# Second parts of 36 weight slabs: an accumulating DMA in place of a VectorE subtraction

## Chip, cores and metric

One core of one Trainium2 chip runs the whole program. The metric is device time in microseconds (us), as the median of several runs; a profile comes from one further execution.

## What is computed

Two residual blocks act on 256 tokens of width 1024, in float32. The first is a gated linear attention, a convolutional feed-forward, an attention and a second feed-forward. The second block, where the change lies, is cut here to what matters:

```
h = rmsnorm(x) * (1 + scale) + shift
c_val, c_gate, c_og, ts, r_og, g_conv, g_rwkv = split(h @ w_in)
y_conv = (silu(layernorm(conv31(c_val * sigmoid(c_gate)))) * silu(c_og)) @ w_conv_out
y_rwkv = (norm(rwkv7_scan(r, k, v, ... from ts)) * silu(r_og)) @ w_rwkv_out
m = sigmoid(g_conv) * y_conv + sigmoid(g_rwkv) * y_rwkv
x = x + gate * (m @ w_out);  return rmsnorm(x)
```

## The kernel before

**Split weights.** A weight matrix comes in slabs of 128 x 1024 (512 KB). `Weights.load` (L67) loads a slab into `raw` by a DMA that SP issues (L76), ACT rounds it to float32r as `hi` (L77), and DVE makes the remainder `lo = raw - hi` (L78). `mm3` (L107) then issues three matmuls for each of the 8 blocks of a slab: `hi` with the activations' first part (L110), `hi` with their second part (L111), and `lo` with their first part (L112). A slab is 24 matmuls. The third of them already needs `lo`.

**Buffers.** The pools ask for five `raw` tiles (L1239) and three each of `hi` and `lo` (L1240); the build hands out more where SBUF is free. In the addresses of the built programs, slabs of `w_r` and `w_k` reuse the `lo` of four (before) or five (changed) slabs earlier, those of `w_v` and of the gates the one of three slabs earlier.

**Stages of the second block.** `low` and `cvg` are projections; `pr`, `pk` and `pv` project `w_r`, `w_k`, `w_v` (8 slabs each). `prep` builds the scan's chunk matrices. `inv` inverts 32 x 32 triangular blocks on DVE: two transposes (L799), 31 steps of a multiplication (L618, tile `sub`) and an addition (L808), and transposes back (L817, L819). After them TensorE goes on with `zp` (L829), `xp` (L839) and `chain`, four chunks of small matmuls (`u`, `sp`, `op`, `ur`) with copies on ACT and additions on DVE between them and two norms (`ost`, L911). The last stages are `rout`, `cout`, `wout` and `final`.

**What fills the gaps.** Slabs of the gates `rog`, `gr`, `cog` and `gc` (8 each) are given to `prep`, `inv` and `chain` as filler by `fill`, and the 248 taps of the 31-wide convolution (L1017, L1019) fill DVE. `gr`, `cog` and `gc` leave for DRAM through `kept` (an ACT activation, L943, and a DMA that ACT issues, L944) and come back later; `rog` stays in SBUF. The framework's list scheduler sets the order on every engine from its own costs, and each engine works through its order without overtaking. The lines before and after the change differ by five from L78 on (L829 is L834 there).

Of the kernel before, what the change touches and what calls it, by code (L numbers as in the profile page):

```python
# [12 lines left out]
AF = mybir.ActivationFunctionType  # L13
ALU = mybir.AluOpType
# [3 lines left out]
P = 128  # L18
# [40 lines left out]
class Weights:  # L59
# [5 lines left out]
        self.last = None  # L65
        self.ready = {}

    def load(self, src, out=None):

        g, nc = self.g, self.g.nc  # L70
        w, n = src.shape[-1], self.n
        self.n += 1
        raw = g.wraw.tile([P, 1024], F32, tag="raw", name=f"raw{n}")
        hi, lo = out or [g.wsp.tile([P, 1024], F32R, tag=a, name=f"{a}{n}") for a in ("hi", "lo")]
        with g.tc.issue_after(self.last.ins):
            self.last = nc.sync.dma_start(raw[:, :w], src)  # L76
        nc.scalar.copy(hi[:, :w], raw[:, :w])  # L77
        nc.vector.tensor_tensor(out=lo[:, :w], in0=raw[:, :w], in1=hi[:, :w].bitcast(F32), op=ALU.subtract)  # L78
        return hi[:, :w], lo[:, :w]
# [10 lines left out]
        self.last = self.g.nc.sync.dma_start(raw, src)  # L90
        return raw.rearrange("p (k c) -> p k c", c=P)

    def blocks(self, src, n):

        w = self.ready.pop(str(src), None) or self.load(src)
        return [a.rearrange("p (k c) -> p k c", c=n) for a in w]

    def ahead(self, where, i):
# [9 lines left out]
def mm3(nc, ps, lhs, rhs, start, stop):  # L108
    (lh, ll), (rh, rl) = lhs, rhs
    nc.tensor.matmul(ps, lh, rh, start=start, stop=False)  # L110
    nc.tensor.matmul(ps, lh, rl, start=False, stop=False)  # L111
    nc.tensor.matmul(ps, ll, rh, start=False, stop=stop)  # L112
# [63 lines left out]
def scaled(g, w_col, name, wide=T):  # L176

    nc = g.nc
    hh = g.sb.tile([P, KD, wide], F32R, tag=f"ph{wide}", name=f"ph_{name}")
    hl = g.sb.tile([P, KD, T], F32R, tag="pl", name=f"pl_{name}")  # L180
    for k in range(KD):
        nc.scalar.activation(hh[:, k, :T], g.x[:, k, :], AF.Copy, scale=w_col[:, k:k + 1])
        nc.vector.scalar_tensor_tensor(out=hl[:, k, :], in0=g.x[:, k, :], scalar=w_col[:, k:k + 1], in1=hh[:, k, :T].bitcast(F32), op0=ALU.mult, op1=ALU.subtract)
    return hh, hl
# [8 lines left out]
def normed(g, w_col, rstd, name, shift=None):  # L193

    nc = g.nc
    hh, hl = [g.sb.tile([P, KD, T], F32R, tag=t, name=f"{t}_{name}") for t in ("hh", "hl")]
    for k in range(KD):
        h = g.sb.tile([P, T], F32, tag="e", name=f"h_{name}{k}")
        nc.vector.scalar_tensor_tensor(out=h, in0=g.x[:, k, :], scalar=w_col[:, k:k + 1], in1=rstd, op0=ALU.mult, op1=ALU.mult)
        if shift is None:  # L200
            split_act(g, h, hh[:, k, :], hl[:, k, :])
        else:
            s = shift[:, k:k + 1]
            nc.scalar.activation(hh[:, k, :], h, AF.Identity, bias=s)
            nc.vector.scalar_tensor_tensor(out=hl[:, k, :], in0=h, scalar=s, in1=hh[:, k, :].bitcast(F32), op0=ALU.add, op1=ALU.subtract)
    return hh, hl
# [48 lines left out]
        nc.vector.tensor_tensor(out=g.x[:, c, :], in0=ps[:, :T], in1=g.x[:, c, :], op=ALU.add)  # L255


def projecting(g, src, h, evac, first=0, hp=None):


    nc = g.nc
    for c in range(src.shape[0]):
        wh, wl = g.w.blocks(src[c], P)
        ps = g.pj.tile([P, 512], F32, tag="pj", name=f"pj{g.w.n}")
        n = T + 2 if c < first else T
        for k in range(KD):
            if c < first:
                nc.tensor.matmul(ps[:, :n], wh[:, k, :], hp[0][:, k, :n], start=k == 0, stop=False)
                nc.tensor.matmul(ps[:, :T], wh[:, k, :], hp[1][:, k, :], start=False, stop=False)
                nc.tensor.matmul(ps[:, :n], wl[:, k, :], hp[0][:, k, :n], start=False, stop=k == KD - 1)  # L270
            else:
                mm3(nc, ps[:, :T], (wh[:, k, :], wl[:, k, :]), (h[0][:, k, :], h[1][:, k, :]), k == 0, k == KD - 1)
        evac(c, ps[:, :n])
        yield


def project(*a, **k):
    for _ in projecting(*a, **k):
        pass
# [310 lines left out]
def head_rows(g, r, name):  # L590

    nc = g.nc
    ps = g.po.tile([16, T], F32, name=f"hr_{name}")
    for t in range(2):
        nc.tensor.transpose(ps[:, t * P:(t + 1) * P], r[:, t, :], g.cst["ident"])
    out = [g.sb.tile([16, T], F32R, tag=f"hr{i}", name=f"hr{i}_{name}") for i in range(2)]
    split_act(g, ps, *out)
    return out
# [15 lines left out]
def second(g, order):  # L614
    nc, I, cst = g.nc, g.I, g.cst
# [9 lines left out]
    hp = scaled(g, wn, "s", T + 32)  # L625
# [3 lines left out]
    h = normed(g, wn, rstd, "s", shift=g.mod)  # L629
# [8 lines left out]
    wl = sb.tile([65, T], F32, name="wl")  # L638
    al = sb.tile([64, T], F32, name="al")
    nc.gpsimd.memset(wl, 1.0)  # L640
    v = Ctx()

    def shift_mix(ps, c, out):
        nc.scalar.activation(out, ps, AF.Copy, scale=mu1[:, c:c + 1])
        nc.vector.scalar_tensor_tensor(out=out[:, 1:], in0=ps[:, :T - 1], scalar=mu[:, c:c + 1], in1=out[:, 1:], op0=ALU.mult, op1=ALU.add)

    def heads(name, after=None):
        v.hexp = sb.tile([16, D], F32R, name="hexp" + name)
        hx = sb.tile([16, D], F32, tag="hx", name="hx" + name)
        with g.tc.issue_after(g.w.last.ins if after is None else after.ins):  # L650
            nc.sync.dma_start(hx, I["hexp"])
        nc.scalar.copy(v.hexp, hx)
# [30 lines left out]
    def pair():  # L683
        if not hasattr(v, "qr"):
            v.qr = sb.tile([P, KD, 2, T], F32, name="qr")

    def pk():
        pair()
        st = psum.tile([P, 2, 16], F32, name="kst")

        def ev(j, ps):
            k = v.qr[:, j, 0, :]
            shift_mix(ps, 8 + j, k)
            sq = sb.tile([P, T], F32, tag="kksq", bufs=LAG + 1, name=f"kksq{j}")
            nc.scalar.activation(sq, k, AF.Square, scale=cst["k_k"][:, j:j + 1])
            sqs.append((j, sq))
            if len(sqs) > LAG:
                norms()

        def norms():  # L700
            j, sq = sqs.pop(0)
            for t in range(2):
                nc.tensor.matmul(st[:, t, 2 * j:2 * j + 2], sq[:, t * P:(t + 1) * P], cst["hind"], start=True, stop=True)

        sqs = []
        project(g, I["w_k"], h, ev)
        while sqs:
            norms()
        heads("k")
        v.rs = head_rows(g, rsqrt(g, st, 1e-24, None, "kk"), "kk")  # L710

    def pr():
        pair()
        project(g, I["w_r"], h, lambda j, ps: shift_mix(ps, j, v.qr[:, j, 1, :]))

    def pv():
        v.VU = sb.tile([P, 4, 16, 64], F32, name="VU")
        v.vf = full("vf")

        def ev(j, ps):  # L720
            vj = v.vf[:, j, :]
            shift_mix(ps, 16 + j, vj)
            vt = psum.tile([P, 4, P], F32, name=f"vt{j}")
            for c in range(4):
                nc.tensor.matmul(vt[:64, c, :], vj[:, c * 64:(c + 1) * 64], cst["center"], start=True, stop=True)
            nc.scalar.copy(v.VU[:64, :, 2 * j:2 * j + 2, :], vt[:64].rearrange("p c (h v) -> p c h v", h=2))

        project(g, I["w_v"], h, ev)


    def prep():
# [199 lines left out]
    def kept(name, src, f):  # L931

        if name not in SPILL:
            t = full(name)
            setattr(v, name, lambda j: t[:, j, :])
            setattr(v, name + "t", t)
            yield from projecting(g, src, h, lambda j, ps: nc.scalar.activation(t[:, j, :], ps, f))
            return
        d = g.dram.tile([P, KD, T], F32, name=name + "d")

        def ev(j, ps):
            t = sb.tile([P, T], F32, tag="spill", bufs=2, name=f"{name}o{j}")
            nc.scalar.activation(t, ps, f)  # L943
            nc.scalar.dma_start(d[:, j, :], t)  # L944

        def get(j):
            t = sb.tile([P, T], F32, tag=name + "i", name=f"{name}i{j}")
            g.w.after(t, d[:, j, :])
            return t

        setattr(v, name, get)
        yield from projecting(g, src, h, ev)

    gates = dict(gr=kept("gr", I["w_gr"], AF.Sigmoid), gc=kept("gc", I["w_gc"], AF.Sigmoid),
                 cog=kept("scog", I["w_cog"], AF.Silu), rog=kept("srog", I["w_rog"], AF.Silu))

# [107 lines left out]
    def wout():  # L1064
# [3 lines left out]
        def ev(j, ps):  # L1068
            nc.vector.scalar_tensor_tensor(out=g.x[:, j, :], in0=ps, scalar=g.mod[:, 16 + j:17 + j], in1=g.x[:, j, :], op0=ALU.mult, op1=ALU.add)

        (project if isinstance(v.mh, list) else project_plain)(g, I["w_out"], v.mh, ev)

    steps = dict(low=low, pk=pk, pr=pr, pv=pv, prep=prep, inv=inv, chain=chain, gains=gains, cvg=cvg, conv=conv, cln=cln,
                 rout=rout, cout=cout, wout=wout)
    for n in order.split():
# [230 lines left out]
```

## Time and profile before

| what | value |
|---|---|
| median of 3 runs | 1025.53 us (1023.55 to 1026.45) |
| profiled execution | 1027.12 us |
| its span, first to last instruction | 1025.3 us |
| TensorE busy | 990.1 us, 97% |
| VectorE busy | 799.8 us, 78% |
| ScalarE busy | 602.8 us, 59% |
| GpSimd busy | 8.4 us, 1% |
| slab DMAs of `w_gr` | 512 KB each, 3.3 us to landing |

The profiled execution has 1.8 us outside its span, and lies 1.6 us above the median of the runs. A busy share is an average over all stages. What a part of the change is worth is read from the stage where it lies: a table of stretches, then the waits and the order of time within one stretch.

### The profile page before, as it was taken

The numbers are of one execution on the slowest core, as the hardware profiler recorded it, in microseconds if no ns is written. First come the engines' busy times: TensorE is split into PE (matmuls) and PEld (weight loads), VectorE is DVE, ScalarE is ACT, GpSimd is POOL, SyncE is SP. The second block draws the span as 40 slices with busy tenths as digits, with TensorE's granted clock in tenths as the row PEclk, the third lists the DMA queues.
The fourth block names the chain that finished last, engine by engine and source line by source line (L and its number), as shares of the span: only waits on it lengthen the run. The fifth ranks groups of instructions, "written<-read, shape, count | busy, mean of one in ns | idle before, by whom it ended". The sixth has DMA issues, their size and how long they took to land. (4 is left out here: it accounts for less than half of the span.)

```text
span 1025.3 us, 20257 instructions
## 1 busy us (share of the span) xinstructions
PE 990.1 (97%) x8124; PEld 940.7 (92%) x8124; DVE 799.8 (78%) x1521; ACT 602.8 (59%) x1057; POOL 8.4 (1%) x19
## 2 busy tenths in 40 slices
PE   6799999999999999899999999999999999999996
PEld 6788899999999878899999998999988898888996
DVE  6765589888876697888887558999898999774674
ACT  7744667666544577656665446545559764634453
POOL 0000000000000000000000000000000100000000
PEclk9899999999999999989999999999999999889998
DMA  7537256556676652365555665455322267313741
GB/s 290 184 131 263 76 175 206 185 187 184 211 258 229 240 189 86 141 205 186 177 187 154 188 243 203 145 185 167 124 85 81 81 222 235 112 37 109 265 161 41
DMA packets 54157, 175.06 MB, mean 171 GB/s; under 512 B 6288, under 2 KB 12944, under 8 KB 53680
## 3 DMA queue, kind: packets, MB, share of 16 engines
q1 hardware_dynamic: 50320, 169.51, 49.8%
q10 hardware_dynamic: 3744, 4.27, 1.2%
q8 instruction: 63, 1.03, 0.4%
q14 instruction: 30, 0.25, 0.1%
HBM read 168.51 MB, written 5.24 MB: 169 GB/s over the span
## 5 line engine op out<-in xcount | busy, mean ns | idle before, releaser
L78 DVE TENSOR_TENSOR lo<-raw,hi 128x1024 fp32r<-128x1024 f32 (+2 forms) x278 | 332.2, 1203 | 28.5 <-ACT hi L77 24.1
L77 ACT CAST hi<-raw 128x1024 fp32r<-128x1024 f32 (+2 forms) x278 | 281.8, 1030 | 41.5 <-PE pj L111 28.5
L112 PE MATMUL up<-hh_f,lo 128*128 128x256 f32 x640 | 182.3, 285 | 2.6 <-DVE lo L78 2.4
L110 PE MATMUL up<-hh_f,hi 128*128 128x256 f32 x640 | 182.4, 285 | 0.8 <-ACT hi L77 0.8
L111 PE MATMUL up<-hl_f,hi 128*128 128x256 f32 x640 | 182.2, 285 | 0.0
L110 PE MATMUL pj<-hh_s,hi 128*128 128x256 f32 x544 | 158.6, 292 | 0.0
L111 PE MATMUL pj<-hl_s,hi 128*128 128x256 f32 x544 | 157.3, 289 | 0.0
L112 PE MATMUL pj<-hh_s,lo 128*128 128x256 f32 x544 | 156.9, 289 | 0.0
L112 PEld LDWEIGHTS up<-hh_f,lo 128*128 128x128 f32 x640 | 124.0, 194 | 3.1 <-DVE lo L78 3.0
L110 PEld LDWEIGHTS up<-hh_f,hi 128*128 128x128 f32 x640 | 124.1, 194 | 1.0 <-ACT hi L77 1.0
L111 PEld LDWEIGHTS up<-hl_f,hi 128*128 128x128 f32 x640 | 124.1, 194 | 0.0
L110 PEld LDWEIGHTS pj<-hh_s,hi 128*128 128x128 f32 x544 | 106.1, 195 | 1.8 <-issue 0.8
L111 PEld LDWEIGHTS pj<-hl_s,hi 128*128 128x128 f32 x544 | 106.3, 195 | 1.0 <-issue 0.3
L112 PEld LDWEIGHTS pj<-hh_s,lo 128*128 128x128 f32 x544 | 106.2, 195 | 1.1 <-issue 0.5
L1019 DVE SCALAR_TENSOR_TENSOR y<-u,long,y 128x255 f32<-128x255 f32 (+27 forms) x240 | 100.1, 473 | 0.2
L110 PE MATMUL dn<-gh,hi 128*128 128x256 f32 x352 | 99.4, 283 | 0.0
L112 PE MATMUL dn<-gh,lo 128*128 128x256 f32 x352 | 99.4, 283 | 0.0
L111 PE MATMUL dn<-gl,hi 128*128 128x256 f32 x352 | 99.4, 283 | 0.0
L238 ACT ACTIVATE y<-up,const 128x256 f32<-128x256 f32 x80 | 45.2, 566 | 51.1 <-PE up L112 46.6
L111 PEld LDWEIGHTS dn<-gl,hi 128*128 128x128 f32 x352 | 67.5, 192 | 0.0
L110 PEld LDWEIGHTS dn<-gh,hi 128*128 128x128 f32 x352 | 67.5, 192 | 0.0
L112 PEld LDWEIGHTS dn<-gh,lo 128*128 128x128 f32 x352 | 67.5, 192 | 0.0
(463 smaller groups left out, 1960.0 us busy)
## 6 DMA issues: line engine op xcount, KB each, us to landing
raw<-w_up SPq DMA_DIRECT2D x88, 512.0 KB, 3.5
raw<-w_down SPq DMA_DIRECT2D x32, 448.0 KB, 3.8
adaw<-ada_w SPq DMA_DIRECT2D x24, 512.0 KB, 4.6
raw<-w_down SPq DMA_DIRECT2D x16, 512.0 KB, 4.5
raw<-w_cvg SPq DMA_DIRECT2D x16, 512.0 KB, 3.4
raw<-gla_v SPq DMA_DIRECT2D x8, 512.0 KB, 5.4
raw<-gla_g SPq DMA_DIRECT2D x8, 512.0 KB, 4.2
raw<-gla_out SPq DMA_DIRECT2D x8, 512.0 KB, 5.0
```

Source lines behind the costliest of these rows:

```text
L77: nc.scalar.copy(hi[:, :w], raw[:, :w])
L78: nc.vector.tensor_tensor(out=lo[:, :w], in0=raw[:, :w], in1=hi[:, :w].bitcast(F32), op=ALU.subtract)
L110: nc.tensor.matmul(ps, lh, rh, start=start, stop=False)
L111: nc.tensor.matmul(ps, lh, rl, start=False, stop=False)
L112: nc.tensor.matmul(ps, ll, rh, start=False, stop=stop)
L238: nc.scalar.activation(yb, ps[:, b, :], AF.Identity, scale=cw[:, 1, c:c + 1], bias=cw[:, 3, c:c + 1])
L1019: nc.vector.scalar_tensor_tensor(out=y[:, i:], in0=u[:, :T - i], scalar=w[:, j, 30 - i:31 - i], in1=y[:, i:], op0=ALU.mult, op1=ALU.add)
```

## The change

In 36 of the 89 split slabs of the second block `lo` is made another way: ACT writes the slab, negated and rounded to float32r, into `lo`, and a DMA issued by POOL (GpSimd) adds `raw` to it. The rounded negative is `-hi`, so the sum is the same remainder. ACT still makes `hi`. With `acc=2` it is every second slab of `w_k`, `w_r` and `w_v` (12), with `acc=1` every slab of those gates that `kept` spills, `gr`, `cog` and `gc` (24). `rog`, which stays in SBUF, and all other slabs keep the subtraction.

```diff
-    def load(self, src, out=None):
+    def load(self, src, out=None, acc=False):
...
             self.last = nc.sync.dma_start(raw[:, :w], src)
+        if acc:
+            nc.scalar.activation(lo[:, :w], raw[:, :w], AF.Copy, scale=-1.0)
+            nc.gpsimd.dma_start(lo[:, :w], raw[:, :w], accum_op=ALU.add)
+            nc.scalar.copy(hi[:, :w], raw[:, :w])
+            return hi[:, :w], lo[:, :w]
         nc.scalar.copy(hi[:, :w], raw[:, :w])
...
-def projecting(g, src, h, evac, first=0, hp=None):
+def projecting(g, src, h, evac, first=0, hp=None, acc=0):
...
-        wh, wl = g.w.blocks(src[c], P)
+        wh, wl = g.w.blocks(src[c], P, acc > 0 and c % acc == acc - 1)
...
-        project(g, I["w_k"], h, ev)
+        project(g, I["w_k"], h, ev, acc=2)
...
-        yield from projecting(g, src, h, ev)
+        yield from projecting(g, src, h, ev, acc=1)
```

`w_r` and `w_v` get `acc=2` in the same way.

The scheduler's order moves with it. On DVE, in the middle of `inv` (`sub` and `LT` are its steps, `y` a convolution tap), before:

```order
L618 TENSOR_TENSOR sub_9448<-LT 128x192
L78 TENSOR_TENSOR lo_9768<-raw_9766,hi_9767 128x1024
L808 TENSOR_TENSOR LT<-LT,sub_9448 128x24x8
L1019 SCALAR_TENSOR_TENSOR y<-u,long,y 128x241
L618 TENSOR_TENSOR sub_9483<-LT 128x207
L1019 SCALAR_TENSOR_TENSOR y<-u,long,y 128x240
L808 TENSOR_TENSOR LT<-LT,sub_9483 128x23x9
L78 TENSOR_TENSOR lo_9837<-raw_9835,hi_9836 128x1024
```

and now:

```order
L623 TENSOR_TENSOR sub_9460<-LT 128x192
L1024 SCALAR_TENSOR_TENSOR y<-u,long,y 128x233
L813 TENSOR_TENSOR LT<-LT,sub_9460 128x24x8
L1024 SCALAR_TENSOR_TENSOR y<-u,long,y 128x232
L623 TENSOR_TENSOR sub_9495<-LT 128x207
L1024 SCALAR_TENSOR_TENSOR y<-u,long,y 128x231
L813 TENSOR_TENSOR LT<-LT,sub_9495 128x23x9
L1024 SCALAR_TENSOR_TENSOR y<-u,long,y 128x230
```

Between the transposes of `inv` there were 19 subtractions and 41 taps; now there are no subtractions and 49 taps. On TensorE, 473 slab matmuls stood between the last matmul of `prep` and the first of `zp`; now there are 311 (46 of `rog`, 265 of spilled gates, some 11 slabs). The other 162 stand among the steps of `chain`, which had 149 and has 311.

On ACT, three gate slabs (`gro` is the gate's output, `grd` its place in DRAM), before:

```order
L943 ACTIVATE gro_10004<-pj_9979 128x256
L944 DMA grd<-gro_10004 128x256
L77 CAST hi_10191<-raw_10190 128x1024
L943 ACT_TABLE_LOAD
L943 ACTIVATE scogo_10082<-pj_10057 128x256
```

and now:

```order
L948 ACTIVATE gro_9814<-pj_9789 128x256
L78 ACTIVATE lo_9994<-raw_9992 128x1024
L80 CAST hi_9993<-raw_9992 128x1024
L949 DMA grd<-gro_9814 128x256
L80 CAST hi_10072<-raw_10071 128x1024
L948 ACTIVATE gro_9884<-pj_9859 128x256
L78 ACTIVATE lo_10073<-raw_10071 128x1024
```

The negation of a slab stands behind the gate activation of the slab three earlier, whose end frees its `lo`. On TensorE, around the first `ost` of `chain`, before:

```order
L886 MATMUL op_10354<-qr,S_10136 64x64 x16
L856 MATMUL ur_10472<-S_10351,qr 64x64
L856 MATMUL ur_10473<-S_10351,qr 64x64
...
L911 MATMUL ost_10424<-long,gsq_10422 128x2 x8
```

and now:

```order
L891 MATMUL op_10380<-qr,S_10158 64x64 x16
L115 MATMUL pj_10421<-hh_s,hi_10415 128x256
L116 MATMUL pj_10421<-hl_s,hi_10415 128x256
L117 MATMUL pj_10421<-hh_s,lo_10416 128x256
...
L916 MATMUL ost_10451<-long,gsq_10449 128x2 x8
```

Fifteen slab matmuls now stand directly ahead of it, as they already do ahead of the second `ost` of the kernel before.

## Rows read from the trace of the kernel before

**Rows 1.** The page's busy time of each engine.

```profile
PE 990.1 (97%) x8124; PEld 940.7 (92%) x8124; DVE 799.8 (78%) x1521; ACT 602.8 (59%) x1057; POOL 8.4 (1%) x19
```

**Rows 2.** Table of stretches of the second block.

```profile
core 0: us, PE busy (x) PEld busy (x) DVE busy (x) ACT busy (x) POOL busy (x), PEclk, DMA share, GB/s
650.00:757.00 107.00, 107.00 (x882) 104.71 (x880) 101.20 (x204) 53.44 (x80) 0.00 (x0) 1.00 0.48 162
...
811.00:869.00 58.00, 56.85 (x473) 56.65 (x473) 57.92 (x128) 32.53 (x48) 0.00 (x0) 1.00 0.66 206
...
872.50:940.60 68.10, 66.81 (x1026) 60.67 (x1026) 42.67 (x88) 30.96 (x53) 0.00 (x0) 0.85 0.22 71
...
876.00:882.30 6.30, 6.30 (x31) 6.01 (x30) 6.30 (x17) 5.29 (x8) 0.00 (x0) 0.51 0.69 220
...
904.00:912.20 8.20, 8.20 (x57) 7.17 (x58) 4.75 (x13) 5.64 (x9) 0.00 (x0) 0.50 0.21 65
912.20:940.60 28.40, 28.01 (x355) 25.02 (x355) 14.58 (x31) 8.48 (x17) 0.00 (x0) 0.99 0.14 46
```

**Rows 3.** Waits from 811 to 872: who waited for whom, total us, times, longest.

```profile
ACT hi L77 <- PE pj L111: 21.6, 15, 1.7
...
PE zp L829 <- DVE X L817: 2.4, 1, 2.4
```

**Rows 4.** The chain that ended last, around `zp` and the end of `chain`.

```profile
872.45 3.62 PE zp L829 x124
...
876.58 0.21 PE pj L112
...
940.64 4.37 PE pj L289 x19
```

**Rows 5.** DVE's groups of instructions from 810 to 872.4.

```profile
L78 DVE TENSOR_TENSOR lo<-raw,hi 128x1024 fp32r<-128x1024 f32 x19 | 23.1, 1218 | 0.0
```

**Rows 6.** DVE in order of time within `inv`: start, us, instruction.

```profile
833.60 1.21 DVE L78 TENSOR_TENSOR lo<-raw,hi 128x1024 fp32r<-128x1024 f32 x1
834.74 0.40 DVE L808 TENSOR_TENSOR LT<-LT,sub 128x240 f32<-128x240 f32 x1
835.06 0.45 DVE L1019 SCALAR_TENSOR_TENSOR y<-u,long,y 128x236 f32<-128x236 f32 x1
835.43 0.40 DVE L618 TENSOR_TENSOR sub<-LT 128x247 f32<-128x247 f32 x1
...
868.32 4.08 DVE L817 STREAM_TRANSPOSE X<-LT 32x1024 f32<-32x1024 f32 x2
```

**Rows 7.** The last matmul of `prep`, tile `nl`: ns min/median/max, first and last start.

```profile
L782 PE MATMUL nl<-VU,lk x128: 218/218/267, 765.7 to 810.7; 64*64 64x64 f32 x128
```

**Rows 8.** ACT in order of time, one gate slab.

```profile
829.01 0.38 ACT L943 ACTIVATE gro<-pj 128x256 f32<-128x256 f32 x1
829.41 0.33 ACTq L944 DMA_DIRECT2D grd<-gro  x1
830.93 1.05 ACT L77 CAST hi<-raw 128x1024 fp32r<-128x1024 f32 x1 [1.55 <-PE pj L111]
```

**Rows 9.** DMA queue of SP (MB, share of 16 engines), and issues with us to landing.

```profile
q1 hardware_dynamic: 50320, 169.51, 49.8%
...
raw<-w_gr SPq DMA_DIRECT2D x8, 512.0 KB, 3.3
raw<-w_cog SPq DMA_DIRECT2D x8, 512.0 KB, 4.8
...
raw<-w_out SPq DMA_DIRECT2D x8, 512.0 KB, 7.1
```

**Rows 10.** ACT's copy behind each `w_v` slab, tile `vt`: first and last start.

```profile
L726 ACT COPY VU<-vt x8: 579/580/583, 730.5 to 760.6; 64x512 f32<-64x512 f32 x8
```

**Rows 11.** TensorE in order of time: the two `ost` of `chain`.

```profile
901.40 2.49 PE L911 MATMUL ost<-long,gsq 128*128 128x2 f32 x16 [0.83 <-ACT gsq L908]
...
928.68 1.90 PE L911 MATMUL ost<-long,gsq 128*128 128x2 f32 x16
```

More of the change, by code (lines that the diff above doesn't have):

```diff
@@ L91, in plain, with blocks @@
         return raw.rearrange("p (k c) -> p k c", c=P)
-    def blocks(self, src, n):
-        w = self.ready.pop(str(src), None) or self.load(src)
+    def blocks(self, src, n, acc=False):
+        w = self.ready.pop(str(src), None) or self.load(src, acc=acc)
         return [a.rearrange("p (k c) -> p k c", c=n) for a in w]
@@ L713, in pr @@
         pair()
-        project(g, I["w_r"], h, lambda j, ps: shift_mix(ps, j, v.qr[:, j, 1, :]))
+        project(g, I["w_r"], h, lambda j, ps: shift_mix(ps, j, v.qr[:, j, 1, :]), acc=2)
     def pv():
@@ L726, in ev @@
             nc.scalar.copy(v.VU[:64, :, 2 * j:2 * j + 2, :], vt[:64].rearrange("p c (h v) -> p c h v", h=2))
-        project(g, I["w_v"], h, ev)
+        project(g, I["w_v"], h, ev, acc=2)
     def prep():
```

## The prediction

> **What bounds the kernel now.** The first view is the page's busy time [rows 1]: TensorE works 97% of the span, VectorE (DVE) 78%. That alone says that a relief of DVE pays only where TensorE waits for DVE. The second view, the table of stretches [rows 2], looks for such places in the second block. From 650 to 757 us (`w_r`, `w_k` and half of `w_v`) TensorE has no idle time at all, though DVE too is busy 101.2 of 107 us. From 811 to 869 it runs 473 slab matmuls in 56.85 us, 0.12 us each or 2.88 us per slab, at full clock, beside a DVE that is busy 57.92 of 58.00 us. Both engines are full there. The waits of that stretch [rows 3] show two things. ACT waits 15 times, 21.6 us in all, for TensorE before it writes a `hi`: the buffers of a gate slab come free only when TensorE ends an earlier slab. And TensorE waits once for DVE, 2.4 us, for the transposes that end `inv`. From there the chain that ended last [rows 4] goes through `zp` at 872.45 and the chunks of `chain` to the first large group of `rout` at 940.64. In those 68.1 us TensorE is idle for only 1.3 us [rows 2]. So little idle time is to be had anywhere: TensorE's work is only moved about, and what else can be won is clock. In two pieces, 876 to 882.3 and 904 to 912.2, the granted clock is 0.51 and 0.50, which is the lower level (1.2 GHz): a slab matmul comes every 0.21 us [rows 4].
>
> **DVE in `inv`.** The 19 subtractions leave [rows 5]. In the stream one takes 833.60 to 834.74, 1.14 us, and a tap 835.06 to 835.43, 0.37 us [rows 6]. Eight more taps stand there now. 19 x 1.14 - 8 x 0.37 = 18.7 us: the transposes end at 853.7 in place of 872.4, and `zp` can begin 18.7 us earlier if TensorE is there by then. The 12 subtractions that leave `w_r`, `w_k` and `w_v` are worth nothing: TensorE is full in that stretch [rows 2], and their place is taken by taps.
>
> **TensorE ahead of `zp`.** `prep` ends at 811 [rows 7]. Behind it stand 46 matmuls of `rog`, 46 x 0.12 = 5.5 us, and about 11 spilled slabs. With three buffers, the time from the end of a slab to its buffer being ready again, L, sets the pace: (L + 2.88) / 3 per slab if that is above 2.88, so from L = 5.76 on.
>
> **L, which no row shows.** After a slab ends, ACT does the gate activation (0.38 us) and the negation; the cast of the same shape on ACT takes 1.05 us [rows 8], and I take that. Then POOL issues the DMA; handing over to it has no row, and I put it between 0 and 1 us, and take 0.3. The DMA itself is bounded from below by the load of the same 512 KB, 3.3 us for `w_gr` [rows 9]. From above: it must read `lo` besides `raw`, so at worst it is as two transfers one after the other in a crowded stage, 7.1 (`w_out`) and 4.8 (`w_cog`), 11.9 us. In engine time a slab is 0.498 x 1025.3 us / 169.51 MB x 0.524 MB = 1.6 us of all 16 DMA engines [rows 9]. The nearest case is one landing and a second reading, 3.3 + 1.6 = 4.9 us. L = 0.38 + 1.05 + 0.3 + 4.9 = 6.6 us, the pace is 3.16 us, and 5.5 + 11 x 3.16 = 40.3 us put TensorE at 851.3, just ahead of DVE's 853.7. So this wait is covered by `inv`, with 2.4 us to spare; from L = 7.3 on `zp` is late, and if that cover is gone altogether it costs 11 x 0.28 = 3.1 us.
>
> **The other 12.** In `w_r` and `w_k` five buffers give 4 x 2.88 = 11.5 us, above 6.6. In `w_v` a slab comes every (760.6 - 730.5) / 7 = 4.3 us [rows 10], and three buffers give 8.6 us. Both are taken at 0. POOL's own work (memsets and small copies) stands ahead of the 24 gate DMAs, so nothing on POOL waits behind them. SP issues the next load of a `raw` later, when the accumulation has read it; five buffers at 2.88 us cover that.
>
> **`chain`.** The 162 moved matmuls cost 162 x 0.12 = 19.4 us there. Against that, fifteen of the slab matmuls now stand ahead of the first `ost`. Before, TensorE waited 0.83 us at that place for ACT, and behind it came the 8.2 us at half clock; ahead of the second `ost` 15 slab matmuls stood already, there was no wait [rows 11], and the clock stayed at 0.99 [rows 2]. I take both as removed: 0.8 us, and half of 8.2, 4.1 us. ACT gets nine more casts and some 13 negations in `chain`, about 22 x 1.05 = 23 us, where it is busy 31.0 of 68.1 us [rows 2]. Its copies for the scan can stand behind one of them; with ten such copies that is 0 to 10 us, and I take 2, since TensorE has slabs to do meanwhile.
>
> **Sum.** -18.7 + 19.4 - 0.8 - 4.1 + 2.0 = -2.2 us against the profiled execution of 1027.1 us. That execution lies 1.6 us above the median of the runs; the same difference on the median gives 1025.5 - 2.2 = **1023.3 us**. The rest of the program is unchanged: after 940 TensorE has the same work in the same order. No change is what a measurement can't tell within about 0.3%, 3.1 us here.
>
> **A rule that speaks against it.** From 811 to 869 the DMA engines are already busy 0.66 of the time [rows 2]. In the 42.7 us that are left ahead of `zp`, 11 loads and 11 accumulations of 1.6 us each take 35 us, and with the second reading 53 us. The Trainium skill ("DMA: Bandwidth & Descriptors", section on issuing engines not being separate DMA queues) says that DMAs issued by SP, ACT and POOL all run on the same 16 engines and interleave. By that rule the accumulations take their time from the loads, and the time is that of the first rival below; by the landings of the loads alone it is the 1023.3 above. No row here has a DMA of POOL in it.
>
> **Rivals.**
> - **The DMA engines fill, and `lo` comes late (slower).** Landing 3.3 + 4.8 = 8.1 us, L = 9.8, pace 4.2: 5.5 + 11 x 4.2 = 51.7 us, so `zp` at 862.7, 9.0 us later than DVE allows; in `w_v` (9.8 - 8.6) / 2 x 4 = 2.4 us. -2.2 + 9.0 + 2.4 = +9.2: **1034.7 us**. It decides from L = 7.3. For it: the 53 us of engine time above. Against: the loads land in 3.3 us at that load. At the upper bound of 11.9 us (L = 13.6, pace 5.5) TensorE needs 66.0 us in place of 42.7 ahead of `zp`, 23.3 us more, with 10 in `w_v` and some 8 in `w_r` and `w_k`: +39 us, 1064 us.
> - **The clock stays up in all of `chain` (faster).** With twice the slabs between the small matmuls, the 6.3 us at half clock behind `zp` go as well, and ACT costs nothing: -2.2 - 3.2 - 2.0 = -7.4: **1018.1 us**. For it: the full clock from 912 on. Against: `zp` with its 128 tiny matmuls still comes first, behind a wait for DVE.
> - **The moved slabs only stand in front of `chain` (slower).** Pieces of 36 to 48 matmuls now stand ahead of steps of the scan. If the low clock stays and ACT's extra work costs 4 us: -18.7 + 19.4 + 4.0 = +4.7: **1030.2 us**.
> - **It does nothing**: the remainder is made by either engine in time and the order makes up for it. That is within the forecast.
>
> **Chances.** The forecast has 0.45 with a spread of some 4 us: 0.14 of it faster by over 0.3%, 0.27 within, 0.04 slower. Late `lo`: 0.30 (0.28 slower, 0.02 within). Clock: 0.18, faster. Slabs in front: 0.07, slower. Together faster 0.32, within 0.29, slower 0.39. The range goes from 1017 (just below the clock's case) to 1043; above that lies about a third of the late `lo`, whose landing would be near its upper bound, and below it the best of the clock's case. The forecast's own range is 1019 to 1028.
>
> **What would show it.** Right: the transposes of `inv` end near 854, `zp` starts with them, 36 DMAs of POOL land in about 5 us, TensorE waits little for them, and the clock from the first `ost` on is full. Wrong: TensorE's waits for POOL's DMAs are the longest in the table of waits; a gate slab takes 4 us or more; loads of `w_cog` land later than 4.8 us; `chain` from `zp` to `rout` takes well over 68.1 + 16.5 = 84.6 us.

## The result, and the profile after

The changed kernel takes **1054.7 us** (median of 4 runs, 1049.6 to 1056.8) against 1025.7 us of the kernel before on the same chip (4 runs, 1023.6 to 1026.5). The ratio is **1.0273**, 95% interval 1.0251 to 1.0294: slower, and outside the range that was given. The profiled execution took 1055.9 us, its span is 1054.1 us, 28.8 us above that of before.

The page of the changed kernel, to be held against [rows 1] and [rows 9]: busy time, then TensorE's third matmul of a slab with the idle time ahead of it, then the DMA queues (packets, MB, share of 16 engines), then issues with their median time to landing.

```profile
PE 999.6 (95%) x8124; PEld 946.1 (90%) x8124; DVE 760.1 (72%) x1485; ACT 636.2 (60%) x1093; POOL 37.4 (4%) x55
...
L117 PE MATMUL pj<-hh_s,lo 128*128 128x256 f32 x544 | 161.1, 297 | 22.7 <-DMA lo<-raw 22.7
...
q1 hardware_dynamic: 50320, 169.51, 47.6%
q0 software_dynamic: 5184, 18.88, 9.6%
...
lo<-raw POOLq DMA_DIRECT2D x36, 512.0 KB, 6.5
...
raw<-w_gr SPq DMA_DIRECT2D x8, 512.0 KB, 3.9
raw<-w_cog SPq DMA_DIRECT2D x8, 512.0 KB, 5.9
```

VectorE is relieved by 40 us, as the change says. But TensorE now waits 22.7 us for `lo<-raw`, a wait that did not exist before, and q0 is a new queue: 0.096 x 1054.1 us / 36 = **2.8 us of all 16 DMA engines for each accumulation**, while a load of the same 512 KB still takes 0.476 x 1054.1 / 169.51 x 0.524 = 1.55. Half of them need over 6.5 us to land.

Table of stretches of the changed kernel, columns as in [rows 2]; the third goes from the end of `zp` to the first large group of `rout`.

```profile
650.00:757.00 107.00, 101.93 (x819) 99.15 (x819) 94.57 (x214) 58.75 (x85) 10.37 (x12) 0.98 0.71 198
...
821.00:869.00 48.00, 37.94 (x277) 35.95 (x278) 46.16 (x119) 28.94 (x40) 9.46 (x11) 0.94 0.95 230
...
881.50:967.40 85.90, 79.12 (x1059) 73.39 (x1052) 15.83 (x33) 48.79 (x75) 8.59 (x10) 0.90 0.75 204
```

In the first stretch TensorE was never idle before [rows 2]; now it is for 5 us. In the inversion (821 to 869) the DMA engines are busy 0.95 of the time, and TensorE runs 277 matmuls, of which 263 belong to slabs. The first 46 of these are `rog`'s, which were not changed; they run at the old pace and are through at 826.8. From there on 217 slab matmuls take 40.6 us (without 1.6 us of six others among them), 40.6 / 217 x 24 = 4.5 us per slab in place of 2.88. The granted clock, 1.00 in the inversion before [rows 2], is 0.94 over this stretch: behind some of the waits it falls to the lower level (1.2 GHz), as from 850 to 853, where it is 0.57 and 18 matmuls run, against 27 in the same time before.

Landmarks of the changed kernel, to be held against [rows 4, 6, 7]: the last matmul of `prep` and `zp` (first and last start), and VectorE's transposes that begin and end the inversion (start, us).

```profile
L787 PE MATMUL nl<-VU,lk x128: 218/218/366, 775.0 to 821.1; 64*64 64x64 f32 x128
...
820.62 4.09 DVE L804 STREAM_TRANSPOSE LT<-VU 64x1024 f32<-64x1024 f32 x2
861.52 4.15 DVE L822 STREAM_TRANSPOSE X<-LT 32x1024 f32<-32x1024 f32 x2
...
L834 PE MATMUL zp<-X,VU x128: 191/191/212, 878.3 to 881.5; 32*32 32x32 f32 x128
```

VectorE ends the inversion at 865.7, and `zp` comes 12.6 us later: nothing on VectorE holds it any more, TensorE isn't there yet. The waits of TensorE in 811 to 882, against [rows 3], and four pieces of the chain that ended last, against [rows 4], say for what it is late:

```profile
PEld pj L117 <- DMA lo<-raw: 14.1, 9, 2.7
PE pj L117 <- DMA lo<-raw: 12.1, 9, 2.5
```

```profile
865.34 8.94 DMA lo<-raw
...
878.60 9.09 DMA lo<-raw
...
945.29 9.20 DMA lo<-raw
...
967.45 7.61 PE pj L294 x34
```

The chain now goes through landings of 9 us. `rout` starts at 967.45 in place of 940.64.

### The profile page after: what moved, and what is told of

It reads as the page before. It is cut to its first block, busy times and chain, and to the rows that moved or that the text cites. A ratio compares the mean times of both kernels' runs of the same rounds, so it can differ in the third digit from the quotient of the medians.

```text
span 1054.1 us, 20330 instructions
## 1 busy us (share of the span) xinstructions
PE 999.6 (95%) x8124; PEld 946.1 (90%) x8124; DVE 760.1 (72%) x1485; ACT 636.2 (60%) x1093; POOL 37.4 (4%) x55
## 3 DMA queue, kind: packets, MB, share of 16 engines
q1 hardware_dynamic: 50320, 169.51, 47.6%
## 4 chain that ended last, share of the span: by engine, by line
PE 77%; DMA 7%; DVE 6%; issue 5%; ACT 3%; POOL 0%; DVEq 0%; POOLq 0%; ACTq 0%
PE up L117 8%; PE up L115 8%; PE up L116 8%; PE pj L115 6%; PE pj L117 6%; DMA lo<-raw 6%; PE pj L116 6%; PE dn L115 4%; PE dn L116 4%; PE dn L117 4%; PE pj L294 3%; PE pt L115 2%; PE pt L117 2%; PE pt L116 2%; DVE y L1024 2%
## 5 line engine op out<-in xcount | busy, mean ns | idle before, releaser
L83 DVE TENSOR_TENSOR lo<-raw,hi 128x1024 fp32r<-128x1024 f32 (+2 forms) x242 | 287.5, 1198 | 27.5 <-ACT hi L82 25.1
L82 ACT CAST hi<-raw 128x1024 fp32r<-128x1024 f32 (+2 forms) x242 | 244.1, 1027 | 12.0 <-issue 5.8
L117 PE MATMUL pj<-hh_s,lo 128*128 128x256 f32 x544 | 161.1, 297 | 22.7 <-DMA lo<-raw 22.7
L115 PE MATMUL pj<-hh_s,hi 128*128 128x256 f32 x544 | 161.0, 296 | 0.0
L115 PEld LDWEIGHTS pj<-hh_s,hi 128*128 128x128 f32 x544 | 108.7, 200 | 1.5 <-issue 0.3
L1024 DVE SCALAR_TENSOR_TENSOR y<-u,long,y 128x240 f32<-128x240 f32 (+27 forms) x240 | 99.1, 459 | 0.0
```

Source lines behind the costliest of these rows:

```text
L1024: nc.vector.scalar_tensor_tensor(out=y[:, i:], in0=u[:, :T - i], scalar=w[:, j, 30 - i:31 - i], in1=y[:, i:], op0=ALU.mult, op1=ALU.add)
```

## The experiments

All runs in one table; the ratios are to the kernel before on the same chip, the three columns behind them from the profiled executions. S is taken as the start of the second block (the first matmul of a tile `pj` that reads `hh_s`), then comes the span less S. This column is needed because the build lays out the buffers of all stages anew for every program: four programs reach S 7 to 10 us later, a time that lies ahead of everything the edits touch. In the addresses of these four built programs `hi` and `lo` repeat after three slabs from the start of the program on, in the others after four or five. The last three columns stand on one execution each, and such an execution lies up to 6 us from the median of its kernel's runs (`all_copy`; 3.3 us in `gates_only`), so a difference of a few us between two rows is not shown by them.

| kernel | accumulations | ratio (95%) | S | span - S | against before |
|---|---|---|---|---|---|
| before | none | 1 | 632.5 | 392.8 | |
| changed | 12 + 24 | 1.0273 (1.0251 to 1.0294) | 633.7 | 420.4 | +27.6 |
| proj_only | 12 | 1.0092 (1.0064 to 1.0120) | 633.6 | 401.6 | +8.8 |
| gates_only | 24 | 1.0219 (1.0181 to 1.0257) | 631.3 | 412.4 | +19.6 |
| all_copy | 36 copies | 1.0068 (1.0032 to 1.0103) | 633.9 | 403.1 | +10.3 |
| neg_only | no transfer | 0.9948 (0.9931 to 0.9965) | 631.3 | 387.4 | -5.4 |
| gates_buf5 | 24 | 1.0202 (1.0167 to 1.0237) | 632.5 | 414.1 | +21.3 |
| gates_noload | 24 | 1.0137 (1.0105 to 1.0170) | 639.5 | 397.9 | +5.1 |
| idle_dma | 24 unused | 1.0343 (1.0310 to 1.0375) | 642.5 | 417.9 | +25.1 |
| gates_half | 12 of gates | 1.0248 (1.0221 to 1.0276) | 639.6 | 407.9 | +15.1 |
| half_early | 12 of gates | 1.0138 (1.0107 to 1.0170) | 640.9 | 397.3 | +4.5 |
| proj_early | 12 | 1.0039 (1.0021 to 1.0057) | 631.6 | 398.3 | +5.5 |
| grcog_early | 8 of gates | 1.0065 (1.0052 to 1.0079) | 631.3 | 398.7 | +5.9 |
| gates_pool | none, GpSimd | 1.0289 (1.0262 to 1.0316) | 631.7 | 422.1 | +29.3 |

**Which stage pays.** Two runs split the change.

```diff
-        project(g, I["w_k"], h, ev, acc=2)
+        project(g, I["w_k"], h, ev, acc=0)
```

(the same for `w_r` and `w_v`), and for the other run

```diff
-        yield from projecting(g, src, h, ev, acc=1)
+        yield from projecting(g, src, h, ev, acc=0)
```

> The 12 accumulations of w_k, w_r and w_v go back to subtractions on VectorE; the 24 of the gates stay. Theory (two separate costs): prep of the changed kernel ended 10.4 us late (821.1 against 810.7) because TensorE lost that time in w_k, w_r and w_v; without them prep ends near 811 and the time is 1054.7 - 10.4 = about 1044 us. Rival (the delay ahead of prep would be caught up later, because the gates' DMAs set the end of the stage): the time stays within 3 us of 1054.7.

> The counterpart: accumulations in w_k, w_r and w_v alone, the gates' slabs subtracted on VectorE again. Theory: the 12 cost TensorE about 10 us there and nothing catches it up, since VectorE sets the end of the inversion: 1025.7 + 10 = about 1036 us. Rival (VectorE, relieved of 12 subtractions, is ahead by prep and makes it up): 1026 to 1029 us, no difference to the kernel before.

Measured: 1048.9 and 1036.5 us. The 12 accumulations of `w_k`, `w_r` and `w_v` cost what was expected; with the gates alone `prep` does end at 809.7 again, but the time is 5 us above the 1044. In the block the two losses add up (8.8 + 19.6 = 28.4 against 27.6; by the ratios 0.9% and 2.2% against 2.7%), so within the scatter they are separate, and the gates carry two thirds.

**What the transfer costs.** The third run makes a plain copy of each accumulation, the fourth leaves the transfer out.

```diff
-            nc.gpsimd.dma_start(lo[:, :w], raw[:, :w], accum_op=ALU.add)
+            nc.gpsimd.dma_start(lo[:, :w], raw[:, :w].bitcast(F32R))
```

```diff
-            nc.gpsimd.dma_start(lo[:, :w], raw[:, :w], accum_op=ALU.add)
+            pass
```

> The same 36 DMAs from raw to lo, as a plain copy in place of an adding one; the negation stays and so does the order of all instructions. lo then holds the slab itself, so the remainder is left out of the computation. Theory (the adding is what is dear): from 811 to 970 us an accumulation took 0.426 x 159 / 24 = 2.8 us of all 16 DMA engines, a load of the same 512 KB 1.5; a plain copy takes about 1.5, the landing comes down from a median of 6.5 us to 4 or less, and the time is near 1030 us. Rival (any DMA that POOL issues is so slow, or the extra bytes alone fill the engines): landing above 6 us and the time within 4 us of 1054.7.

> The 36 DMAs are left out, the negation on ScalarE stays: lo holds the negated slab, so the remainder is left out of the computation. It is the changed kernel with transfers that cost nothing. Theory (the transfers are the whole of the loss): prep ends near 811, the transposes that end the inversion near 854, zp starts there, and the time is what the prediction's sum gives without its wait for landings, 1020 to 1026 us. Rival (the extra work of ScalarE and the 162 matmuls that are moved behind the inversion cost as well): 1030 us or more.

The queue of the copies and the landings of the 12 copies of `w_k`, `w_r` and `w_v`; then the landings of the same 12 in the changed kernel, and the queue of the run with the 24 accumulations of the gates alone:

```profile
q0 software_dynamic: 5184, 18.88, 5.1%
...
DMA to landing us min/median/max: 2.9/3.7/4.8
```

```profile
DMA to landing us min/median/max: 4.6/5.6/8.8
...
q0 software_dynamic: 3456, 12.58, 6.5%
```

A copy takes 0.051 x 1037.0 / 36 = 1.47 us of the engines, a load's price; adding makes 0.065 x 1043.7 / 24 = 2.83 of it. With the copies `prep` ends at 812.7, as long after S as before, so there nothing is late any more, and the block loses 10.3 us in place of 27.6. The expected 1030 was missed by little (1032.5 us median, in runs from 1025.9 to 1041.0; the profiled execution is among the longer ones). The 24 copies of the gates land in 5.1 us (median), above the 4 that were expected. Of the kernel without transfers:

```profile
849.50 4.06 DVE L822 STREAM_TRANSPOSE X<-LT 32x1024 f32<-32x1024 f32 x2
...
L834 PE MATMUL zp<-X,VU x128: 191/236/249, 851.5 to 856.9; 32*32 32x32 f32 x128
```

The transposes end at 853.56, `zp` follows at once, and the time is 1020.9 us. So the transfers are the whole loss, and what the relief of VectorE is worth with transfers that cost nothing is 0.5% (0.3 to 0.7).

**Full engines, or too few buffers?** The run of the gates alone, with five `lo`:

```diff
-        hi, lo = out or [g.wsp.tile([P, 1024], F32R, tag=a, name=f"{a}{n}") for a in ("hi", "lo")]
+        hi, lo = out or [g.wsp.tile([P, 1024], F32R, tag=a, bufs=5 if a == "lo" else 3, name=f"{a}{n}") for a in ("hi", "lo")]
```

> The gates alone accumulate, and lo has five buffers in place of three (8 KB more per partition). Theory A (the DMA engines are full: share 0.95 from 821 to 869): more buffers only let more accumulations queue up; landings grow, and the time is within 3 us of the run with three buffers, about 1044. Theory B (the prediction's own formula: three buffers and a hand-over L of 9.8 us set the pace of a slab, (L + 2.88) / 3 = 4.2 us): with five the pace is (9.8 + 2.88) / 5 = 2.5, below TensorE's 2.88, so TensorE is not held, the inversion ends by VectorE's work near 854, and the time is 1020 to 1027 us.

Stretch 811 to 869, the landings from 811 to 970 and two waits from 811 to 882, first of the gates alone, then with five buffers:

```profile
811.00:869.00 58.00, 47.25 (x342) 44.67 (x341) 45.24 (x129) 35.03 (x46) 12.21 (x14) 0.94 0.99 247
...
lo<-raw POOLq DMA_DIRECT2D x24, 512.0 KB, 7.6
...
DVE X L822 <- DMA scogd<-scogo: 12.7, 1, 12.7
...
PE pj L117 <- DMA lo<-raw: 10.8, 9, 2.9
```

```profile
811.00:869.00 58.00, 47.58 (x368) 45.71 (x364) 44.26 (x129) 39.83 (x56) 12.07 (x14) 0.94 1.04 263
...
lo<-raw POOLq DMA_DIRECT2D x22, 512.0 KB, 8.9
...
DVE X L822 <- DMA scogd<-scogo: 13.7, 1, 13.7
...
PE pj L117 <- DMA lo<-raw: 8.8, 6, 3.9
```

The time is the same (1048.6 against 1048.9 us). In the built program the negation then stands three or four slabs ahead of its use in place of two for nearly all of the 24, and the landings grow with the engines full. Theory B falls: the slabs ahead of `zp` come every 3.8 us on average in place of 4.0, far from its 2.88, and TensorE is through with them at 867.4, not near 854. So buffers help little where the engines are full, though more than the equal time says. Over the whole block TensorE's waits for `lo` halve, from 17.2 to 8.8 us, and other waits come in their place: TensorE waits 3.7 us for the transposes that end the inversion, and 5.4 us for ScalarE at the first `ost`. The transposes stand ready at 855 (853 with three buffers) and wait until 869 (866) for `scogd<-scogo`, the transfer of a spilled gate's output to DRAM: in both built programs their tile `X` lies on addresses of such an output. In the changed kernel it does not, and this wait is not there; in three of the runs below it takes 2.4 to 4.3 us. What five buffers give without it, no run shows. The next run takes the loads away:

```diff
-        raw = g.wraw.tile([P, 1024], F32, tag="raw", name=f"raw{n}")
+        raw = g.same if acc else g.wraw.tile([P, 1024], F32, tag="raw", name=f"raw{n}")
...
-        with g.tc.issue_after(self.last.ins):
-            self.last = nc.sync.dma_start(raw[:, :w], src)
+        if not acc:
+            with g.tc.issue_after(self.last.ins):
+                self.last = nc.sync.dma_start(raw[:, :w], src)
```

> The gates alone accumulate all 24 slabs, but 24 slab loads are left out: every gate slab is made from one tile loaded once, so the gates' weights are left out of the computation. The order of work and the place of the negations stay, the DMA engines lose 24 x 1.5 = 36 us of work of the 110 they have between 811 and 970 us. Theory A (full engines make the landings long): share near 0.65, landings near the shortest seen, 4.5 us, so L = 0.38 + 1.05 + 0.3 + 4.5 = 6.2 us against two slabs of 5.8, and the time is 1020 to 1029 us. Theory B (two slabs of lead are too few for an accumulation at any load): landings of 5 us or more and 1036 us or more.

```profile
811.00:869.00 58.00, 51.69 (x409) 47.98 (x408) 53.53 (x147) 40.86 (x62) 12.54 (x15) 0.97 0.72 153
...
lo<-same POOLq DMA_DIRECT2D x24, 512.0 KB, 5.3
```

(`g.same` is a tile into which one slab is loaded ahead of the gates.) The landings fall from 7.6 to 5.3 us, TensorE's waits for `lo` from 17.2 to 7.3, and the block's loss from 19.6 to 5.1 us. The whole time, 1039.8 us, hides it: 7 us of it lie ahead of the block. By the numbers as they were put down theory B is met (landings of 5 us or more, 1036 us or more); without the 7 us the time lies between the two theories. As far as this one run tells, the crowded engines carry some three quarters of the gates' loss, and lateness at a lighter load the rest (0.38 + 1.05 + 0.3 + 5.3 = 7.0 us against two slabs of 5.8). The split is rough, since the run takes away every wait for a load too. The Trainium skill ("DMA: Bandwidth & Descriptors", section on issuing engines not being separate DMA queues) says that transfers issued from ScalarE, SyncE or GpSimd run on the same 16 engines and interleave. By these two pairs the trace agrees: shares of 0.99 and 1.04 are the sum of SP's and POOL's transfers, and without SP's loads POOL's landings come down.

Then the accumulations alone, into a tile that nobody reads, beside the old subtraction:

```diff
+            no = g.wsp.tile([P, 1024], F32R, tag="no", bufs=2, name=f"no{n}")
+            nc.scalar.activation(no[:, :w], raw[:, :w], AF.Copy, scale=-1.0)
+            nc.gpsimd.dma_start(no[:, :w], raw[:, :w], accum_op=ALU.add)
```

> As with the gates alone, but the 24 negations and accumulations go to a spare tile that nobody reads, and lo comes from the subtraction on VectorE as in the kernel before. Nothing waits for these DMAs; they only use the engines and hold raw until they have read it. Theory A (the DMA engines are full): the loads and the release of raw are delayed, slabs come at 3.5 to 4.2 us in the inversion though lo no longer waits, fewer of them fit ahead of zp, and the time is 1035 to 1050 us. Theory B (only the lateness of lo costs): nobody waits, so the time is that of the kernel before, 1025 to 1029 us.

1061.5 us, of which 10 lie ahead of the block: without these, just above theory A's range. No engine uses the result, yet the block loses 25.1 us. The waits from 811 to 875 show how:

```profile
ACT no L79 <- DMA no<-raw: 15.6, 6, 5.1
...
DVE lo L82 <- ACT hi L81: 10.0, 4, 4.7
PEld pj L114 <- ACT hi L81: 4.6, 2, 3.2
```

ScalarE waits for the two spare tiles, and behind that wait in its queue stand the casts for which VectorE and TensorE wait. So this run isn't contention alone, as it was meant to be; its two tiles added a wait of their own.

**The place of the negation.** In the changed kernel's order on ScalarE (numbered names; `pj244` is the gate slab whose evacuation this is, `lo246` belongs to the slab of `pj247`):

```
868 L948 ACTIVATE gro5_9884<-pj244_9859 128x256
869 L78 ACTIVATE lo246_10073<-raw246_10071 128x1024
...
872 L948 ACTIVATE gro6_9954<-pj245_9929 128x256
873 L78 ACTIVATE lo247_10108<-raw247_10106 128x1024
```

The negation stands behind an evacuation that waits for TensorE, so the time to its use is that of the slabs `pj245` and `pj246`, 2 x 2.88 = 5.8 us. The gates' `lo` buffers repeat after three slabs; in `w_k` and `w_r` they repeat after five, and there too only two slabs stand between for 11 of the 12 accumulated ones of `w_k`, `w_r` and `w_v`. One run takes half of the gates' accumulations, two ask for accumulated slabs earlier (these two with four `lo` buffers):

```diff
-        yield from projecting(g, src, h, ev, acc=1)
+        yield from projecting(g, src, h, ev, acc=2)
```

```diff
-        wh, wl = g.w.blocks(src[c], P, acc > 0 and c % acc == acc - 1)
+        wh, wl = early.pop(c, None) or g.w.blocks(src[c], P, acc > 0 and c % acc == acc - 1)
+        for e in range(c + 1, min(c + 4, src.shape[0])):
+            if acc > 0 and e % acc == acc - 1 and e not in early:
+                early[e] = g.w.blocks(src[e], P, True)
```

> The gates accumulate every second slab (12 DMAs in place of 24), w_k, w_r and w_v none. DMA engine time per slab in the inversion falls from 2.83 + 1.5 + 0.3 (spilled outputs) = 4.6 us to 3.2, near TensorE's 2.88. Theory A (engine time): TensorE is hardly held, VectorE's relief of some 9 us shows, and the time is 1022 to 1031 us. Rival (each accumulated slab is late by itself, whatever the load): half of the loss of 22.9 us stays, about 1037 us.

> Accumulations in w_k, w_r and w_v alone, each accumulated slab asked for up to three slabs earlier, lo with four buffers. In the instruction order of the changed kernel its negation stands on ScalarE behind the evacuation of the slab three ahead of it, so two slabs, 2 x 2.88 = 5.8 us, are left for evacuation (0.47), negation (1.05), hand-over and a landing of 5.4: some 7.2 us; now three to five slabs are between, 8.6 to 14.4 us. Theory (ScalarE's place for the negation makes it late): TensorE no longer waits there, and the time is 1025 to 1030 us in place of 1036.5. Rival (the bursts on the DMA engines delay it whatever the place): 1034 us or more.

> Every second gate slab accumulates, as in the run with half the accumulations (1051.6 us), but each accumulated slab is asked for up to three slabs earlier and lo has four buffers: three or four slabs stand between the negation and the use, 8.6 to 11.5 us, in place of two. Theory (with the DMA engines at 0.66 it was lateness by order, handed on to ScalarE's casts and through them to VectorE's remaining subtractions): the lateness goes and VectorE's relief shows, 1020 to 1031 us. Rival (the engine time of the transfers, or VectorE's subtractions waiting in its queue, whatever the place of the negation): 1040 us or more.

Half of the gates (1051.6 us, 7 of them ahead of the block) is a clear miss: the block still loses 15.1 us, with the engines at 0.66, no more than before the change. Its stretch and waits:

```profile
811.00:869.00 58.00, 50.43 (x407) 47.99 (x408) 48.88 (x121) 35.94 (x60) 6.42 (x8) 0.94 0.66 180
```

```profile
PE pj L117 <- DMA lo<-raw: 9.1, 5, 3.4
...
DVE lo L83 <- ACT hi L82: 8.5, 3, 5.6
ACT hi L82 <- PE pj L116: 8.5, 4, 3.6
```

Read from the top: TensorE waits five times, 1.8 us each, for an accumulated slab; ScalarE's next cast waits for TensorE; and VectorE, which still makes the other remainders, waits for the cast with the whole inversion behind it in its queue. From its first to its last transposes it now takes 64.7 us, no less than the 62.1 of before. With all 24 accumulated VectorE was at least out of this ring. With the longer lead the same 12 lose 4.5 us in place of 15.1, and the 12 of `w_k`, `w_r` and `w_v` 5.5 in place of 8.8 (TensorE waits for `lo` once there, 2.6 us, in place of four times, 4.6). The theory has the direction right, and neither run came down to its number: the 12 of `w_k`, `w_r` and `w_v` take 1031.8 us, those of the gates 1040.1. The latter is where its rival began (1040 us); 8 us of it lie ahead of the block.

**Versions that might win.** The last run keeps what had helped: eight accumulations, in the inversion only, with the longer lead.

```diff
-        yield from projecting(g, src, h, ev, acc=1)
+        yield from projecting(g, src, h, ev, acc=2 if name in ("gr", "scog") else 0)
```

> Accumulations in every second slab of w_gr and w_cog alone (8 DMAs), asked for up to three slabs earlier, lo with four buffers; w_gc, whose slabs come behind the inversion, and w_k, w_r and w_v keep the subtraction. The lead is three slabs or more, and in the inversion the DMA engines get some 5 x 2.8 = 14 us of work more, where 0.34 x 58 = 20 us were free. Theory (the loss was full engines and too short a lead; both are gone): VectorE is relieved of four or five subtractions ahead of the end of the inversion, 5 us, which are given back as slabs behind it; with the run without transfers 5.5 us below the kernel before as the bound, the time is 1022 to 1028 us, no measurable difference. Rival (VectorE's remaining subtractions wait in its queue for casts that wait for late slabs, at any number of accumulations): 1030 us or more.

1033.6 us, between the two. Asked for early, all eight are issued from 812 to 855 together with the loads:

```profile
811.00:869.00 58.00, 50.66 (x401) 49.61 (x400) 50.92 (x129) 33.41 (x46) 7.04 (x8) 0.95 0.92 250
...
DMA to landing us min/median/max: 4.9/8.2/9.4
...
PE zp L837 <- DVE X L825: 3.9, 1, 3.9
...
DVE lo L83 <- ACT hi L82: 3.7, 2, 3.4
...
866.13 4.03 DVE L825 STREAM_TRANSPOSE X<-LT 32x1024 f32<-32x1024 f32 x2 [3.24 <-DMA scogd<-scogo]
```

The engines are full again, at 0.92. The waits (from 811 to 880) and the line of the transposes that end the inversion say where VectorE's relief goes: VectorE loses 3.7 us to late casts and 3.2 to the transfer of a spilled gate on whose addresses `X` lies here too. From its first to its last transposes it takes 61.0 us, 1.1 less than before, and TensorE waits 3.9 us for it, against 3.0 for `lo`. And the subtraction on GpSimd, without any transfer:

```diff
+            nc.scalar.copy(hi[:, :w], raw[:, :w])
+            nc.gpsimd.tensor_tensor(out=lo[:, :w], in0=raw[:, :w], in1=hi[:, :w].bitcast(F32), op=ALU.subtract)
```

> The 24 subtractions of the gates go to GpSimd as one tensor_tensor each, without negation and without DMA. No row of a run shows what 128x1024 takes there. If it is at most 2.9 us and VectorE is not slowed, the inversion ends near 854, the DMA engines stay at the load of before, and the time is 1018 to 1026 us. If GpSimd takes 4 us or more per slab, it sets the pace in place of the DMA: 1035 us and more; or if VectorE's own instructions become longer beside it, the inversion ends no earlier than before, 1026 to 1035 us.

1055.3 us. GpSimd takes 2.41 us, less than the bound of 2.9, and is still no help. GpSimd's and VectorE's instructions at the same moment (start, us):

```profile
828.25 2.45 POOL L79 TENSOR_TENSOR lo<-raw,hi 128x1024 fp32r<-128x1024 f32 x1 [0.71 <-ACT hi L78]
```

```profile
827.99 0.45 DVE L1023 SCALAR_TENSOR_TENSOR y<-u,long,y 128x238 f32<-128x238 f32 x1
828.36 2.56 DVE L622 TENSOR_TENSOR sub<-LT 128x192 f32<-128x192 f32 x1
830.85 0.45 DVE L1023 SCALAR_TENSOR_TENSOR y<-u,long,y 128x237 f32<-128x237 f32 x1
...
831.87 0.36 DVE L622 TENSOR_TENSOR sub<-LT 128x207 f32<-128x207 f32 x1
```

VectorE's instruction, some 0.36 us by itself (last line), lasts as long as GpSimd's instruction beside it. The relief of 1.14 us a slab is paid with 2.2 for each instruction that is caught so, and the inversion takes 77.9 us from its first to its last transposes in place of 62.1. The Trainium skill ("SBUF — State Buffer", section "Who interferes with whom") says that a VectorE instruction with two SBUF inputs contends with a GpSimd instruction that reads SBUF, because its second input comes through a read interface that the two share. The pair of lines agrees. None of the versions beats the kernel before.

## Why the prediction was wrong, point by point

The forecast was -2.2 us, the profiled execution gave +28.8. By its own steps:

- **(VectorE in the inversion, -18.7.)** Right. From the first to the last transposes it was 810.29 to 872.40, 62.1 us; it is 820.62 to 865.67, 45.05: **-17.1 us**, 1.6 short. Without transfers the transposes end at 853.56, where 853.7 was forecast; that this is so near is luck, since the relief is 1.6 us short there too and the inversion began 1.7 us earlier.
- **(TensorE ahead of `zp`, covered.)** Wrong, and the largest part. From the last `nl` to `zp` 42.8 us were forecast and 57.0 measured, **+14.2 us**: `rog` took its 5.5 us, and the 11 spilled slabs 48.9 (without 2.6 us of ten matmuls of the tile `cmean`, which now stand there too), 4.4 us each in place of 3.16. The step that failed is the size of the landing: 4.9 us was taken as "the nearest case", the gates' accumulations landed in 7.4 (median; 4.5 to 11.5). The other terms of L were right; the hand-over to POOL, which had no row, takes the 0.3 us that were assumed (a negation from 833.53 takes 1.05, POOL issues at 834.88). The shortest accumulation, 4.5, is near the 4.9. But the prediction took the landing of a transfer that has the engines to itself, though its own sum in the part on the rule (35 to 53 us of engine time in 42.7) said that it hasn't. At 2.83 us an accumulation that sum is 11 x (1.6 + 2.83) = 49 us ahead of `zp`, as much as the 11 slabs took. With the landing put right the formula of the three buffers comes near as well: L = 0.38 + 1.05 + 0.3 + 7.4 = 9.1 us, pace (9.1 + 2.88) / 3 = 4.0; the lower clock behind the waits, for which the sum had no term, adds some 0.3 (an estimate: 0.94 for 1.00 over 57.0 us is 3.4 us). Yet it is not the number of buffers that sets the pace in the main, since with five the formula gives no wait at all and the slabs still came every 3.8 us. This is the rival "the DMA engines fill", and its pace of 4.2 was near; it was given 0.30, and its 1034.7 us left out what follows.
- **(The other 12, taken at 0.)** Wrong: **+10.4 us** (`prep` ends at 821.3 in place of 810.9; 1.2 us of this lie ahead of S), +8.8 in the block by themselves. The slack was counted in buffers, 11.5 us (8.6 in `w_v`). The negation's place on ScalarE leaves two slabs, 5.8 us, against 0.47 + 1.05 + 0.3 + 5.4 = 7.2. The order of the built program, which was known, shows it. A lead of three slabs and more took back 3.3 of the 8.8; with the shorter landing of a copy (3.7 us, so 5.5 in sum) `prep` was on time. In the run of these 12 alone not all of the 8.8 us are waits for `lo`, of which TensorE has 4.6 us; the granted clock falls behind them there too (0.83 from 690 to 700).
- **(`chain`, +16.5.)** Direction right, size short by 4.5: from the start of `zp` to `rout` 89.2 us against 68.2 (872.45 to 940.64) + 16.5 = 84.7. The clock did rise (0.85 to 0.90), but TensorE is idle for 6.8 us there, waits for `lo` above all, where the sum had nothing for landings. Behind `rout` another 2.0 us are lost, which no run was made for.
- **The sum**: 14.2 + 10.4 + 4.5 + 2.0 = 31.1, less 2.2, is 28.9 us. With transfers at no cost the remaining terms hold to some 3 us: -2.2 forecast, -0.52% = -5.3 us measured (-3.6 to -7.1).
- **What would show it** was named rightly: TensorE's waits for POOL's transfers are its longest, a gate slab takes 4.4 us, `w_cog` lands in 5.9 us, and the stage from `zp` is over 84.6 us.

What stays open: how the 15 us that half of the gates lose divide between the lateness of each slab and the ring through VectorE; how much of the gates' loss more buffers would take back, since the run with five met a wait of its own; and what eight accumulations with a long lead would cost where `X` does not wait for a spilled gate.

## What to carry to other kernels

A subtraction that moves from a compute engine to a transfer isn't gone: count the DMA engines' time of the stage first, loads and additions together, and take the landing of a full queue if that sum comes near the stage's length. The slack of a buffer is not the number of buffers: it is the work between the place where its first writer stands in its engine's queue and the use, and a writer that stands behind an evacuation gets only the slabs that come after that one. Where only part of a kind of work is moved, look who still does the rest: an engine that keeps half of it waits for the late half too. And a run that comes out the same can hide one wait gone and another come: look at the waits, and at what lies on the addresses of the tile that is waited for, before a theory is dropped.

## What the runs showed of the hardware

- An accumulating transfer of 512 KB within SBUF takes 2.83 us of all 16 DMA engines, a plain one 1.47, a load of the same size 1.5; the shortest landings of the first two are 4.5 and 2.9 us. POOL's issue takes 0.86 us for the one and 0.53 for the other.
- With the engines at 0.95 to 1.04 landings go to 9 us and over, and with five buffers for three they rise (7.6 to 8.9 us), while TensorE's waits for them halve (17.2 to 8.8 us in the block).
- The granted clock falls to the lower level behind waits of TensorE: 0.57 from 850 to 853 in the changed kernel, 18 matmuls in the time of 27.
- A two-input VectorE instruction beside GpSimd's tensor_tensor of 128x1024 (2.41 us) lasts as long as that one: 2.56 us in place of 0.36.
